# Strassen's algorithm for 14 pairs of the first layer's FFN input, and low parts of its FFN output weights by transfers that add

## The chip, the cores and the metric

The kernel runs on one NeuronCore of a Trainium2 chip. The metric is device microseconds of one execution. Engines are called by their names in the profile: PE (TensorE, matmuls), PEld (its weight loads), DVE (VectorE), ACT (ScalarE), POOL (GpSimd) and SP (SyncE, which issues most transfers). SBUF is the on-chip memory, PSUM the accumulators that PE writes.

## The reference

A trunk of two layers on 512 tokens of width 1024, all in float32. Each layer first mixes tokens (a gated recurrence beside latent attention, about half of the time) and then runs the FFN that this change touches:

```python
mod = (c @ w_ada + b_ada)[:, None, :]
sh_m, sc_m, g_m, sh_f, sc_f, g_f = jnp.split(mod, 6, axis=-1)
...
x = x + g_m * (y @ w_out)
h = rms_norm(x) * (1 + sc_f) + sh_f
gate, up = jnp.split(h @ w_ffn_in, 2, axis=-1)
x = x + g_f * ((jax.nn.silu(gate) * up) @ w_ffn_out)
```

`w_ffn_in` is 1024 x 5632 and `w_ffn_out` 2816 x 1024. The six modulation vectors of a layer come from one conditioning vector `c` and the 1024 x 6144 matrix `w_ada`.

## The kernel before, in words

**Numbers in two parts.** PE multiplies float32 operands at a rounded precision (float32r), so every operand is split in a high part (rounded, by ACT) and a low part (what is left, by DVE), and each product is three matmuls: high by high, high by low, low by high (`mm3`). `split` is the pair of instructions; `w_cols` loads a block of weights, 128 x 1024 floats, from HBM into a `raw` tile and splits it into `whi` and `wlo`. There are three `raw` buffers (`NRAW`) and three pairs of `whi` and `wlo` (`NHL`). In the second layer's FFN output (the argument `dma=last`) `w_cols` already makes the low part in another way: ACT writes minus the high part into `wlo`, and a transfer issued by POOL adds `raw` to it.

**The FFN.** `layer` works on 22 pairs: pair number `fi` is a block of 128 gate columns and the 128 up columns that belong to it. The pairs stand in three blocks (`FCUTS`: pairs 0 to 6, 7 to 13, 14 to 21). Pair 0 (`NAHEAD`) is made ahead, while the norm's statistics are still being computed. The next `NPLAIN[l]` pairs are plain: `gemm_units` makes two units, gate and up, each of 8 x 3 matmuls of 512 columns, and `done_fi` multiplies silu(gate) by up and splits the result into `ah` and `al`. The rest go through `fi_pair`, Strassen's algorithm in Winograd's form: the 2 x 2 blocks are (gate, up) by the two halves of the 1024 inputs on the weight side, and the two halves of the inputs by the two halves of the tokens (`H0`, `H1`, 256 each) on the other. `w_quarters` makes the sums of weights and their splits, `token_halves` the sums of tokens and theirs, once for the whole FFN. A pair is then seven products of 4 x 3 matmuls of 256 columns, between which DVE and ACT read the PSUM accumulators `a`, `b` and `z` and add.

Before the change `NPLAIN` is (21, 5): in the first layer all 21 remaining pairs are plain, and the tokens are prepared by `make_h`; in the second pairs 1 to 5 are plain and 6 to 21 Strassen, and the tokens are prepared by `token_halves`.

The output weights follow by blocks (`fo_block`): while block two's pairs run, the 8 output units of block one (7 x 3 matmuls of 512 columns each) are put between them, while block three's run those of block two, and after the last pair come the 8 units of block three (8 x 3 matmuls each), alone. Each unit ends in an update of the residual `x`.

**Modulation tiles.** A modulation vector is eight tiles: a 512 KB block of `w_ada` is loaded into one of two `graw` buffers, and one DVE instruction multiplies it by `c` and sums. Generators of such tiles stand in the list `background`; each call of `bg()` takes one step. `gemm_units` calls `bg()` after each of its units; `fi_pair` does not. A vector takes nine steps for its eight tiles. In the first layer's FFN the list holds seven vectors (this layer's `G_F`, then the second layer's six), and what is left of it is recorded at once by `drain_bg()` before the last output block. With `BG_GATE` a tile's load waits for the last PE instruction that was recorded before it.

**Order of the work.** The kernel's code only records instructions. `Recorder.order` then simulates them with a table of costs and sets the order of each engine's queue: of the instructions that are ready, the one with the most work still behind it goes first. PE keeps nearly the recorded order. `POOL_DMA` and `POOL_LAT` are this planner's figures for a POOL issue and its landing. Since all instructions are issued at the recorder's end, the profile gives every one the same line, L524; it is read by the names of tiles: `fh`, `fl` (tokens of plain pairs), `xqh`, `xql` (tokens of Strassen pairs), `ws`, `wsh`, `wsl` (sums of weights and their parts), `graw` (modulation tiles).

Of the kernel before, what the change touches and what calls it, by code (L numbers as in the profile page):

```python
# [16 lines left out]
AF = mybir.ActivationFunctionType  # L17
ALU = mybir.AluOpType
# [3 lines left out]
P = 128  # L22
# [3 lines left out]
KD = D // P  # L26
# [6 lines left out]
NF = D_FF // P  # L33
# [33 lines left out]
H0, H1, FULL = slice(0, 256), slice(256, 512), slice(0, 512)  # L67
# [4 lines left out]
NGRAW = 2  # L72
NAHEAD = 1
NLATE = (0, 0)
NPLAIN = (21, 5)
BG_GATE = True
TABLES_AT = 4
SCRIPT = ('x4 x0 d0 d1 x1 m1 x5 x2 n0 n1 g0 g1 x3 b0 r0 p0 b5 g2 e0 m1 m1 g3 q0 g4 s0 e4 b1 q1 a3 t0 g5 a1 p1 q2 w0 v0 a0 y0 m1 s1 m1 s2 x6 m1 e3 x7 w4 e1 b2 t2 g6 m1 q3 a2 m1 e2 s3 r1 b3 v2 m1 g7 p2 m1 q5 e7 w3 t3 q4 w2 m1 v3 e6 w7 b7 m1 s4 a5 w6 y2 a7 a4 m1 p3 e5 q6 a6 t1 w1 s6 s5 m1 b4 v1 y3 t5 m1 t4 q7 t6 v4 s7 b6 v6 m1 t7 y6 v5 w5 v7 y1 y5 y4 y7', 'd0 d1 m1 n0 m1 m1 n1 x1 x0 r0 m1 m1 x2 p0 g0 g1 e0 a0 q1 q0 x3 s1 g2 b0 e2 p1 m1 m1 m1 t1 q2 s0 m1 v1 e1 x4 w0 q3 m1 g3 r1 s2 x5 t0 g4 a1 p3 a2 v0 b6 e4 x7 s3 q6 x6 m1 m1 g5 e5 w2 y0 w4 m1 s6 b1 w1 m1 g6 a4 e6 b2 t3 v3 a6 e3 g7 b3 m1 p2 q7 q5 b7 s7 w3 b5 s5 b4 y1 w6 t6 w5 v6 q4 m1 t5 t2 v2 y6 s4 v5 a3 y2 a5 t4 t7 v4 v7 e7 y3 y5 a7 w7 m1 y4 y7')
# [27 lines left out]
DMA_RUN = 0.6  # L106
DMA_LAT = 2400.0
DMA_ISSUE = 470.0
POOL_DMA = 1200.0
POOL_LAT = 6000.0  # L110
SHORT = 2000.0
TABLE_LOAD = 1300.0
PE_WINDOW = 3413.0
# [424 lines left out]
def trunk(  # L538
# [7 lines left out]
    V, A, T, G, DMA = (  # L546
        rec.engine(e, r)
        for e, r in (("DVE", nc.vector), ("ACT", nc.scalar), ("PE", nc.tensor), ("POOL", nc.gpsimd), ("SP", nc.sync))
    )
# [24 lines left out]
    def f(ap):  # L574
        return ap.bitcast(F32)

    def split(hi, lo, src):
        A.activation(hi, src, AF.Copy)
        V.tensor_tensor(lo, src, f(hi), ALU.subtract)
# [12 lines left out]
    def raw_tile():  # L592
        return rec.tile(wp, [P, 1024], F32, "raw", NRAW, nm("raw"))
# [12 lines left out]
            res.append((hi, lo))  # L606
        return res

    def w_cols(src, nk=KD, raws=None, dma=False):


        raw = raw_tile()
        DMA.dma_start(raw[:, : nk * P], src)
        hi, lo = hl_tiles()
        if dma:
            A.activation(hi[:, : nk * P], raw[:, : nk * P], AF.Copy)
            A.activation(lo[:, : nk * P], f(hi[:, : nk * P]), AF.Copy, scale=-1.0)
            G.dma_start(f(lo[:, : nk * P]), raw[:, : nk * P], accum_op=ALU.add)
        else:
            split(hi[:, : nk * P], lo[:, : nk * P], raw[:, : nk * P])  # L620
        if raws is not None:
            raws.extend(raw[:, k * P : (k + 1) * P] for k in range(nk))
        return [(hi[:, k * P : (k + 1) * P], lo[:, k * P : (k + 1) * P]) for k in range(nk)]
# [61 lines left out]
    for i in range(2):  # L685
        ps, crow, cs = psum("pt"), unit("crow"), slice(i * 512, (i + 1) * 512)
# [189 lines left out]
    def w_quarters(srcs):  # L876

        raws = []
        for src in srcs:
            raw = raw_tile()  # L880
            DMA.dma_start(raw, src)
            raws.append(raw)
        lo_, hi_ = slice(0, 512), slice(512, 1024)
        a11, a12, a21, a22 = raws[0][:, lo_], raws[0][:, hi_], raws[1][:, lo_], raws[1][:, hi_]
        s1, s2, s3, s4 = (unit("ws") for _ in range(4))
        res = {}
        h, l_ = hl_tiles()
        split(h, l_, raws[0])
        res["A11"], res["A12"] = (h[:, lo_], l_[:, lo_]), (h[:, hi_], l_[:, hi_])

        def add(name, s):
            res[name] = unit("wsh", F32R), unit("wsl", F32R)
            split(*res[name], s)

        V.tensor_tensor(s1, a21, a22, ALU.add)
        V.tensor_tensor(s2, s1, a11, ALU.subtract)
        add("S2", s2)
        V.tensor_tensor(s3, a11, a21, ALU.subtract)
        add("S3", s3)
        add("S1", s1)  # L900
        add("A22", a22)
        V.tensor_tensor(s4, a12, s2, ALU.subtract)
        add("S4", s4)
        return res
# [144 lines left out]
    def layer(l, rs, ahead):  # L1049
        last = l == L - 1  # L1050
# [6 lines left out]
        def product(w):  # L1057
            ps = psum("mm")
            for k, (wh, wl) in enumerate(w):
                mm3(ps, wh, wl, hh[k], hl[k], k == 0, k == KD - 1)  # L1060
            return ps
# [9 lines left out]
        if l == 0:  # L1071
            for m in range(3):
                done_down(m, FULL, accs[4 + m])
            ps = accs[NFIRST]
        else:
# [7 lines left out]
            ps = psum("mm")  # L1083
# [30 lines left out]
        xi, v, av, lru_w = {}, {}, {}, {}  # L1114
# [53 lines left out]
        def x_lru(n):  # L1168
            if l == 0 and n < 4:
                ps = unit("xl")  # L1170
                A.activation(ps, accs[n], AF.Copy)
            else:
                ps = product(w_cols(w_in[l, n]))
            convs[n] = conv(n, ps)


# [117 lines left out]
        prs, pts, pos, sas, sbs, yhl = {}, {}, {}, {}, {}, {}  # L1294

        def gate(h, off, res):
            ps = product(w_cols(w_in[l, off + h]))
            res[h] = unit("sg")
            A.activation(res[h], ps, AF.Tanh, scale=0.5)
            if off == OFF_GA:  # L1300
                V.tensor_scalar(res[h], res[h], 1.0, None, ALU.add)
# [19 lines left out]
        yh, yl = [yhl[h][0] for h in range(NH)], [yhl[h][1] for h in range(NH)]  # L1321
# [7 lines left out]
        def done_out(m, cs, ps):  # L1329
# [2 lines left out]
            ahead.add(m, cs)  # L1332

        gemm_units(
            [(m, FULL) for m in range(KD)], yh, yl, lambda m: w_cols(w_out[l, m]), done_out,
        )


# [2 lines left out]
        rs = st.finish(FULL, D, sbuf=True)  # L1341
        na, fast = NAHEAD, NPLAIN[l] + NAHEAD < NF
        pgu, cgu = ahead.units([w_fi[l, c0 + i] for i in range(na) for c0 in (0, NF)])
# [72 lines left out]
            split(ah[fi], al[fi], g)  # L1416

        def w_fi_cols(m):
            return w_cols(w_fi[l, m // 2 + (m % 2) * NF])

        def residual(m, cs, ps):
            V.scalar_tensor_tensor(x[m][:, cs], ps[:, cs], mcol(l, G_F, m), x[m][:, cs], ALU.mult, ALU.add)
# [54 lines left out]
        def fo_block(tiles, ms, done):  # L1477

            k0, nk = tiles[0], len(tiles)
            gemm_units(  # L1480
                ms, [ah[i] for i in tiles], [al[i] for i in tiles],
                lambda m: w_cols(w_fo[l, m, :, k0 * P : (k0 + nk) * P], nk, dma=last), done,
            )


# [75 lines left out]
```

## Time and profile before

| | us |
|---|---|
| median of 3 runs | 1330.85 (1329.75 to 1331.48) |
| the profiled execution | 1330.39 |
| its span, first to last instruction | 1328.6 |
| PE busy | 1309.8 (99%) |
| DVE busy | 945.7 (71%) |
| ACT busy | 676.2 (51%) |
| POOL busy | 235.1 (18%) |
| mean granted TensorE clock | 0.998 |

The first layer's FFN runs from about 328 to 676 us, the second's from about 977 to 1313 us. Matmuls are pipelined: the durations that the profile gives to single ones overlap, so what a group of them takes is read from the length of a stretch and their count, not from their busy times.

### The profile page before, as it was taken

How to read it: one execution, taken by the hardware profiler on the slowest of the kernel's cores; microseconds unless marked ns; L12 is line 12 of the kernel's file. 1: busy time of each engine (PE TensorE's matmuls, PEld its weight loads, DVE VectorE, ACT ScalarE, POOL GpSimd, SP SyncE). 2: the span in 40 equal slices, each digit the busy share in tenths (PEclk: the TensorE clock that was granted, in tenths of full speed). 3: DMA queues.
4: the chain of work that ended last, by engine and by line, in shares of the span. 5: the costliest groups of instructions: out<-in, count | busy, mean ns of one | idle time of the engine just before them, and what ended most of it. 6: DMA issues, size and time to landing. Idle time of an engine off the chain costs nothing.

```text
span 1328.6 us, 18151 instructions
## 1 busy us (share of the span) xinstructions
PE 1309.8 (99%) x6788; PEld 1119.4 (84%) x6788; DVE 945.7 (71%) x1625; ACT 676.2 (51%) x1057; POOL 235.1 (18%) x250
## 2 busy tenths in 40 slices
PE   9999999999999999999999999999999999999997
PEld 7787878888888888888888888888888999899986
DVE  7999887897755555555679886666687766667634
ACT  4597676635322222222356867855474544444532
POOL 0414534314000000000211433312400000000011
PEclk9999999999999999999999999999999999999999
DMA  8744344172655555555414231211333444544473
GB/s 291 237 121 152 117 127 143 64 229 104 220 177 181 172 209 176 183 206 172 147 59 149 94 115 64 96 48 48 106 101 109 133 118 135 155 129 134 126 157 109
DMA packets 56012, 186.44 MB, mean 140 GB/s; under 512 B 7026, under 2 KB 7282, under 8 KB 55924
## 3 DMA queue, kind: packets, MB, share of 16 engines
q1 hardware_dynamic: 52468, 173.75, 39.6%
q0 software_dynamic: 3456, 11.54, 4.7%
q8 instruction: 53, 0.87, 0.3%
q14 instruction: 35, 0.29, 0.1%
HBM read 167.44 MB, written 2.10 MB: 128 GB/s over the span
## 4 chain that ended last, share of the span: by engine, by line
PE 88%; DMA 4%; ACT 3%; DVE 2%; SPq 1%; issue 1%; POOL 0%; DVEq 0%; ACTq 0%
PE mm L524 78%; PE s L524 4%; PE o L524 2%; PE pt L524 2%; DMA raw<-in_w_in_dram 1%; DMA raw<-in_w_ada_dram 1%; SPq L524 1%; DMA graw<-in_w_ada_dram 1%; ACT whi L524 1%; ACT L524 0%; DMA raw<-in_w_ffn_in_dram 0%; DVE raw L524 0%; DMA raw<-in_w_first_dram 0%; DMA crow<-in_c_dram 0%; ACT xc L524 0%
## 5 line engine op out<-in xcount | busy, mean ns | idle before, releaser
L524 ACT ACTIVATE whi<-raw 128x1024 fp32r<-128x1024 f32 (+2 forms) x192 | 199.3, 1038 | 434.6 <-PE mm L524 318.1
L524 DVE TENSOR_TENSOR wlo<-raw,whi 128x1024 fp32r<-128x1024 f32 (+1 forms) x167 | 206.9, 1240 | 103.9 <-ACT whi L524 99.9
L524 PE MATMUL mm<-hl,whi 128*128 128x512 f32 x432 | 168.9, 391 | 0.3 <-DVE hl L524 0.3
L524 PE MATMUL mm<-hh,whi 128*128 128x512 f32 x432 | 166.2, 394 | 1.8 <-ACT ri L524 1.4
L524 PE MATMUL mm<-hh,wlo 128*128 128x512 f32 x416 | 161.8, 390 | 0.0
L524 PE MATMUL mm<-al,whi 128*128 128x512 f32 (+1 forms) x360 | 139.1, 386 | 0.0
L524 PE MATMUL mm<-ah,whi 128*128 128x512 f32 (+1 forms) x360 | 138.9, 386 | 0.0
L524 PE MATMUL mm<-ah,wlo 128*128 128x512 f32 (+1 forms) x360 | 138.5, 385 | 0.0
L524 PE MATMUL mm<-fh,whi 128*128 128x512 f32 x336 | 130.5, 389 | 0.0
L524 PE MATMUL mm<-fh,wlo 128*128 128x512 f32 x336 | 130.5, 389 | 0.0
L524 PE MATMUL mm<-fl,whi 128*128 128x512 f32 x336 | 130.4, 389 | 0.0
L524 PEld LDWEIGHTS mm<-hh,whi 128*128 128x128 f32 x432 | 80.9, 188 | 19.0 <-ACT ri L524 1.5
L524 PEld LDWEIGHTS mm<-hl,whi 128*128 128x128 f32 x432 | 81.2, 188 | 17.4 <-DVE hl L524 1.4
L524 PEld LDWEIGHTS mm<-hh,wlo 128*128 128x128 f32 x416 | 78.1, 188 | 16.0
L524 PE MATMUL mm<-xqh,wsl 128*128 128x256 f32 x320 | 90.4, 283 | 0.0
L524 PE MATMUL mm<-xql,wsh 128*128 128x256 f32 x320 | 90.4, 283 | 0.0
L524 PE MATMUL mm<-xqh,wsh 128*128 128x256 f32 x320 | 90.4, 284 | 0.0
L524 DVE CUSTOM_DVE_ANT_0 graw<-graw,cb,cols 128x1024 f32<-128x1024 f32 x64 | 83.4, 1303 | 6.5 <-DMA graw<-in_w_ada_dram 5.7
L524 POOL TENSOR_SCALAR wsa<-raw,mod 128x128 f32<-128x128 f32 x24 | 17.2, 736 | 388.6 <-PE mm L524 339.4
L524 PEld LDWEIGHTS mm<-ah,whi 128*128 128x128 f32 x360 | 67.7, 188 | 13.2
L524 PEld LDWEIGHTS mm<-ah,wlo 128*128 128x128 f32 x360 | 67.7, 188 | 13.2
L524 PEld LDWEIGHTS mm<-al,whi 128*128 128x128 f32 x360 | 67.7, 188 | 12.6
(257 smaller groups left out, 3055.7 us busy)
## 6 DMA issues: line engine op xcount, KB each, us to landing
graw<-in_w_ada_dram SPq DMA_DIRECT2D x88, 512.0 KB, 4.5
raw<-in_w_ffn_in_dram SPq DMA_DIRECT2D x88, 512.0 KB, 3.4
raw<-in_w_in_dram SPq DMA_DIRECT2D x47, 512.0 KB, 3.4
raw<-in_w_ffn_out_dram SPq DMA_DIRECT2D x32, 448.0 KB, 3.5
raw<-in_w_out_dram SPq DMA_DIRECT2D x16, 512.0 KB, 3.4
raw<-in_w_ffn_out_dram SPq DMA_DIRECT2D x16, 512.0 KB, 3.9
wlo<-raw POOLq DMA_DIRECT2D x16, 448.0 KB, 4.4
raw<-in_w_ada_dram SPq DMA_DIRECT2D x8, 512.0 KB, 4.7
```

What stands on the lines that cost most here:

```text
L524: o.call(*(real(v) for v in o.a), **{k: real(v) for k, v in o.k.items()})
```

## The change

`NPLAIN` goes from (21, 5) to (7, 5): in the first layer pairs 1 to 7 stay plain and pairs 8 to 21 go through `fi_pair`, so the tokens are prepared by `token_halves`. `w_cols` gets a letter for how the low part is made in place of the flag: "v" is `split`, "a" is ACT's negated copy and the transfer that adds. `HOW_FO` is "aa", so the first layer's FFN output now makes its low parts as the second layer's did; all other letters are "v", which is what was there. The branch with `G.tensor_scalar` is used by none. Two figures of the planner change.

```diff
-NPLAIN = (21, 5)
+NPLAIN = (7, 5)
...
-POOL_DMA = 1200.0
-POOL_LAT = 6000.0
+
+HOW_IN = "vv"
+HOW_OUT = "vv"
+HOW_FI = "vv"
+HOW_FO = "aa"
+HOW_A1 = "v"
+POOL_DMA = 900.0
+POOL_LAT = 3700.0
...
-    def w_cols(src, nk=KD, raws=None, dma=False):
+    def split_by(how, hi, lo, src):
+
+
+        if how == "v":
+            split(hi, lo, src)
+            return
+        A.activation(hi, src, AF.Copy)
+        if how == "a":
+            A.activation(lo, f(hi), AF.Copy, scale=-1.0)
+        else:
+            G.tensor_scalar(lo, f(hi), -1.0, 1.0, ALU.mult, ALU.mult)
+        G.dma_start(f(lo), src, accum_op=ALU.add)
+
+    def w_cols(src, nk=KD, raws=None, how="v"):
...
-        if dma:
-            A.activation(hi[:, : nk * P], raw[:, : nk * P], AF.Copy)
-            A.activation(lo[:, : nk * P], f(hi[:, : nk * P]), AF.Copy, scale=-1.0)
-            G.dma_start(f(lo[:, : nk * P]), raw[:, : nk * P], accum_op=ALU.add)
-        else:
-            split(hi[:, : nk * P], lo[:, : nk * P], raw[:, : nk * P])
+        split_by(how, hi[:, : nk * P], lo[:, : nk * P], raw[:, : nk * P])
...
-                lambda m: w_cols(w_fo[l, m, :, k0 * P : (k0 + nk) * P], nk, dma=last), done,
+                lambda m: w_cols(w_fo[l, m, :, k0 * P : (k0 + nk) * P], nk, how=HOW_FO[l]), done,
```

## Rows read from the trace of the kernel before

**Rows 1.** The page: span, busy time by engine, and the copies of high parts.

```profile
span 1328.6 us, 18151 instructions
...
PE 1309.8 (99%) x6788; PEld 1119.4 (84%) x6788; DVE 945.7 (71%) x1625; ACT 676.2 (51%) x1057; POOL 235.1 (18%) x250
...
L524 ACT ACTIVATE whi<-raw 128x1024 fp32r<-128x1024 f32 (+2 forms) x192 | 199.3, 1038 | 434.6 <-PE mm L524 318.1
```

**Rows 2.** Busy time by stretch, the FFN of both layers; PEclk is the granted clock.

```profile
core 0: us, PE busy (x) PEld busy (x) DVE busy (x) ACT busy (x) POOL busy (x), PEclk, DMA share, GB/s
...
327.40:404.20 76.80, 76.80 (x342) 63.48 (x341) 50.63 (x69) 26.69 (x34) 0.00 (x0) 1.00 0.55 186
...
404.20:627.90 223.70, 223.70 (x989) 185.29 (x987) 127.00 (x163) 59.16 (x72) 0.00 (x0) 1.00 0.54 186
...
627.90:676.20 48.30, 48.30 (x215) 40.01 (x214) 33.83 (x40) 19.67 (x27) 15.74 (x22) 1.00 0.42 136
...
964.00:1051.40 87.40, 87.40 (x473) 75.83 (x472) 68.62 (x114) 50.71 (x79) 1.91 (x2) 1.00 0.37 116
1051.40:1160.00 108.60, 107.56 (x744) 100.47 (x743) 75.08 (x126) 53.17 (x86) 6.06 (x7) 1.00 0.48 130
```

**Rows 3.** By stretch: output unit, plain pair; then Strassen pair, output unit.

```profile
404.20:408.96 4.76, 4.76 (x23) 3.94 (x22) 3.72 (x5) 1.60 (x2) 0.00 (x0) 1.00 0.48 170
408.96:419.84 10.88, 10.88 (x50) 9.01 (x49) 4.36 (x5) 2.55 (x4) 0.00 (x0) 1.00 0.47 160
1056.19:1066.26 10.07, 10.07 (x85) 10.05 (x84) 7.26 (x13) 5.05 (x8) 0.85 (x1) 1.00 0.59 178
1066.26:1071.05 4.79, 4.79 (x23) 3.96 (x22) 3.53 (x6) 1.67 (x4) 0.00 (x0) 1.00 0.41 109
```

**Rows 4.** Groups of DVE instructions, 1166.5 to 1265.8 us: busy us, mean ns.

```profile
L524 DVE TENSOR_TENSOR wsl<-ws,wsh 128x512 fp32r<-128x512 f32 x24 | 16.2, 686 | 2.5 <-ACT wsh L524 2.3
L524 DVE TENSOR_TENSOR wlo<-raw,whi 128x1024 fp32r<-128x1024 f32 x6 | 7.3, 1222 | 1.3 <-ACT whi L524 1.0
L524 DVE TENSOR_TENSOR sg<-mm,pq 128x256 f32<-128x256 f32 x13 | 5.5, 424 | 14.0 <-PE mm L524 13.9
L524 DVE SCALAR_TENSOR_TENSOR x<-mm,mod,x 128x512 f32<-128x512 f32 x7 | 5.2, 748 | 2.1 <-PE mm L524 2.1
```

**Rows 5.** Groups of DVE instructions, 404.2 to 513 us: modulation tiles.

```profile
L524 DVE CUSTOM_DVE_ANT_0 graw<-graw,cb,cols 128x1024 f32<-128x1024 f32 x16 | 20.5, 1281 | 1.3 <-DMA graw<-in_w_ada_dram 1.1
```

**Rows 6.** By stretch, columns as in rows 2: output projection, second layer's start, first attention.

```profile
271.80:315.10 43.30, 43.30 (x193) 35.87 (x192) 38.14 (x53) 18.70 (x25) 19.98 (x22) 1.00 0.60 191
...
690.00:750.00 60.00, 59.97 (x290) 49.97 (x289) 56.22 (x102) 42.52 (x69) 9.98 (x8) 1.00 0.41 123
750.00:800.00 50.00, 50.00 (x259) 42.77 (x259) 41.20 (x81) 39.20 (x69) 21.14 (x19) 1.00 0.35 106
...
100.00:225.00 125.00, 118.98 (x580) 98.91 (x580) 108.45 (x208) 87.87 (x149) 56.04 (x46) 1.00 0.42 136
```

**Rows 7.** The chain that ended last, 1140 to 1160 us: start, us, what.

```profile
1145.38 5.77 DMA raw<-in_w_ffn_in_dram
...
1153.87 0.28 ACT pq L524
```

**Rows 8.** Instructions that write `wlo`, 1050 to 1290 us: ns min/median/max; us to landing.

```profile
L524 ACT ACTIVATE wlo<-whi x20: 938/942/1062, 1061.7 to 1288.9; 128x896 fp32r<-128x896 f32 x14, 128x1024 fp32r<-128x1024 f32 x6
L524 POOL DMA_DIRECT2D wlo<-raw x19: 855/862/887, 1063.0 to 1284.5; - x19
...
DMA to landing us min/median/max: 4.2/4.5/7.9
```

**Rows 9.** Loads of modulation tiles, 315 to 650 us: issue ns, first and last start.

```profile
L524 SPq DMA_DIRECT2D graw<-in_w_ada_dram x56: 328/425/437, 317.9 to 636.7; - x56
```

**Rows 10.** The same, 267 to 303 us, beside the first layer's output projection.

```profile
L524 SPq DMA_DIRECT2D graw<-in_w_ada_dram x10: 327/328/426, 267.5 to 294.9; - x10
```

**Rows 11.** The same, 0 to 50 us, the kernel's first products.

```profile
L524 SPq DMA_DIRECT2D graw<-in_w_ada_dram x8: 327/328/430, 6.6 to 39.1; - x8
```

More of the change, by code (lines that the diff above doesn't have):

```diff
@@ L887, in w_quarters @@
         h, l_ = hl_tiles()
-        split(h, l_, raws[0])
+        split_by(HOW_A1, h, l_, raws[0])
         res["A11"], res["A12"] = (h[:, lo_], l_[:, lo_]), (h[:, hi_], l_[:, hi_])
@@ L1172, in x_lru @@
             else:
-                ps = product(w_cols(w_in[l, n]))
+                ps = product(w_cols(w_in[l, n], how=HOW_IN[l]))
             convs[n] = conv(n, ps)
@@ L1296, in gate @@
         def gate(h, off, res):
-            ps = product(w_cols(w_in[l, off + h]))
+            ps = product(w_cols(w_in[l, off + h], how=HOW_IN[l]))
             res[h] = unit("sg")
@@ L1334, in layer @@
         gemm_units(
-            [(m, FULL) for m in range(KD)], yh, yl, lambda m: w_cols(w_out[l, m]), done_out,
+            [(m, FULL) for m in range(KD)], yh, yl, lambda m: w_cols(w_out[l, m], how=HOW_OUT[l]), done_out,
         )
@@ L1418, in w_fi_cols @@
         def w_fi_cols(m):
-            return w_cols(w_fi[l, m // 2 + (m % 2) * NF])
+            return w_cols(w_fi[l, m // 2 + (m % 2) * NF], how=HOW_FI[l])
         def residual(m, cs, ps):
```

## The prediction

> **What bounds the kernel now.** I read the page's first part first: of a span of 1328.6 us TensorE is busy for 1309.8, VectorE 945.7 and ScalarE 676.2 [rows 1]. [...] The second layer's FFN prices what the change adds, since it runs the same functions.
>
> **Step 1, the pairs.** The new setting is 7 plain pairs after the one done ahead, so pairs 8 to 21, 14 of them, go from plain to Strassen. A plain pair is 48 matmuls of 512 columns in 10.88 us (227 ns from start to start); a Strassen pair is 84 of 256 columns in 10.07 us (120 ns) [rows 3]. (The counts in the rows also hold a matmul or two that reach in from either side.) Seven eighths of the columns cost 93% of the time, because each matmul carries some 13 ns beside its columns: from the two rows, 2 x 120 - 227. The gain is 14 x 0.81 = 11.3 us. [...]
>
> **Step 2, the seams.** A block of output units (21 matmuls) takes 4.76 us between plain pairs and 4.79 between Strassen pairs [rows 3]; 16 units between pairs make 16 x 0.03 = +0.5 us.
>
> **Step 3, VectorE in the middle of the FFN.** From the rows a Strassen pair needs on VectorE one split of 1024 (1.22), five splits and four sums of 512 (nine of 0.69), five sums of 256 from PSUM (0.42), and the product and the split of the result (0.69 each): 10.9 us [rows 4]. A plain pair needs two splits of 1024 and two operations of 512: 3.8 us [rows 4]. Each output unit costs one residual update (0.75) [rows 4] and calls one modulation tile of the next layer (1.28) [rows 5]; its split goes away (step 4). A pair and a unit then take 10.9 + 0.75 + 1.28 = 13.0 us of VectorE in 10.07 + 4.79 = 14.9 us of PE: 87%, with 1.9 us to spare. ScalarE stays near half: in the second layer it is at 53.2 of 108.6 us with the same work [rows 2].
>
> How much of that makes PE wait is not shown for this mix, so I bound it. Below: in 690 to 750 us VectorE is 94% busy and PE idle 0.03 us, so 0. Above: in 100 to 225 us VectorE is 87% busy, modulation tiles among its work, and PE idle 6.0 of 125 us, 4.8% [rows 6]; of the 229 us that blocks two and three will take (10.88 + 14 x 10.07 + 16 x 4.79 = 228.4) that is 11.0. The nearest row is the second layer's own Strassen stretch: PE idle 1.0 of 108.6 [rows 2], where the chain runs over a weight tile that took 5.8 us to come and ends at the ScalarE copy that PE wanted, which stood behind that tile's own copies [rows 7]. The added tile can hold a PSUM sum back: between a product and the next into the same accumulator PE has 12 matmuls of cover, 1.44 us, and a sum takes 0.42 plus up to 1.28 of waiting, 1.70. So the 18 tiles called in these blocks cost 0.3 us at most now and then; I take 1.0 for them and 1.0 for the wait that the second layer shows, 2.0 us.
>
> The new preparation of the tokens (8 updates of 0.75, 16 splits, 16 sums of 256: 23.7 us, where 16 updates, 12.0, stood) is hidden: in the second layer PE is busy 87.4 of 87.4 us over it [rows 2], and VectorE in block one, 50.6 of 76.8, takes 12 us more; without that cover it would cost those 12.
>
> **Step 4, low parts by adding transfers.** 24 tiles leave VectorE (24 x some 1.2 us) and take a ScalarE copy of 0.94, a POOL issue of 0.86 and a transfer that lands 4.5 us later, at worst 7.9 [rows 8]. PE sees this only as latency: with the high part's copy (1.04 [rows 1]) the set of buffers is held 7.3 us before PE can use it, plus 5.45 us of use (24 x 227 ns) in the last block. Three sets give 16.35 us; 12.8 fits, and with the worst landing 16.2 still does. Price 0; if the cover went, each of the 24 units would wait by the excess. POOL's issue waits for ScalarE's copy, with the rest of POOL's queue behind it: in blocks two and three that is nothing (POOL is idle there today); in the last block it is the shift sums for the next layer (POOL 15.7 of 48.3 us [rows 2]), which can come later by an issue or two and are read only after the 10.9 us of the units made ahead.
>
> **Step 5, what is late next.** Modulation tiles are called once per GEMM unit, and a Strassen pair makes no such call. 56 tiles belong to this FFN [rows 9]; nine calls bring eight. Today 60 calls come before the last block. After the change there are 2 + 12 + 2 + 16 = 32: three vectors and five tiles, 29, are called there, and the other 27 come in one burst at the last block's start. The burst's pace: 10 issues in 27.4 us, 3.04 us each, beside a fully busy PE [rows 10, 6]. The last block (192 x 0.227 = 43.6 us) and the two units made ahead behind it (10.9) hold 54.5 us, so 18 tiles; their VectorE time, 23 us, fits the 14.5 us idle there today [rows 2] plus the 9.8 of the eight splits that go. SP issues one in some 0.4 us [rows 9], 27 in 11 us, between the weight loads; one that finds its buffer taken holds the loads behind it, which is part of the bound that follows. Nine tiles, 11.5 us, run into the second layer's start, where VectorE has 3.8 us idle to 750 us and 8.8 more to 800 [rows 6]. At best that absorbs all (0); at worst 11.5 - 3.8 = 7.7 us come through. The order ranks a tile by the work that follows it, and these are needed only at the second layer's output projection, so they should fill gaps: nearer 0, I take 2.0.
>
> **Step 6, the planner's figures** for POOL transfers change no operation, only the order, that of the second layer's FFN too: the wait of 1.0 us there may go or another come. -1 to +1, I take 0.
>
> **Sum.** -11.3 + 0.5 + 2.0 + 0 + 2.0 = -6.8 us. The profiled execution took 1330.39 us (span 1328.6 and 1.8 around it), 0.46 under the median of 1330.85. 1330.4 - 6.8 = 1323.6.
>
> **The rivals.**
> A. VectorE becomes the bound in blocks two and three: the idle 1.9 us per pair isn't usable, since it waits on PE in between. For: 87% and 4.8% in the first layer's attention [rows 6]. Against: the same functions at 69% lose 1.0 us in all, and 94% loses nothing elsewhere. Price 11.0 in place of 2.0: 1332.6, no change.
> B. The burst collides with the second layer's start: slower. The mechanism is the tiles' pace. At the kernel's start, with VectorE full, eight issues took 32.5 us, 4.64 each [rows 11]; at that pace 12 tiles fit the 54.5 us and 15 spill, 19.2 us of VectorE, of which 3.8 find room: 15.4 us, so 1330.4 - 11.3 + 0.5 + 2.0 + 15.4 = 1337.0. It decides from 12 spilled tiles on (12 x 1.28 - 3.8 = 11.6, against 8.8 gained before it and 2.7 of margin). For: VectorE is 94% busy from 690 to 750. Against: in the first layer's output projection a burst of ten costs PE nothing, and low-ranked tiles can wait.
> C. Halving the columns costs no more per column: a Strassen pair keeps the full eighth, 10.88 x 7/8 = 9.52 us, the gain is 14 x 1.36 = 19.0, and the time 1330.4 - 19.0 + 4.5 = 1315.9. Against: the second layer's matmuls of a pair start 120 ns apart, not 113, in all of its 16 pairs but at the one wait. 2%. [...]
> D. The pairs don't become Strassen, or buffers keep them apart: the condition in the code is plain, and the second layer's longer stretch fits the same 72 buffers; 1%, 1330.
>
> **How the numbers follow.** Forecast 0.74, range of its own 1318.5 to 1328 (bounds of steps 3, 5 and 6, not all at once); A 0.12, B 0.11, C 0.02, D 0.01. The likeliest time is 1323.5. The range for 8 in 10 takes the forecast's and reaches into A, whose price may be less than its bound: 1318 to 1331. A measurement here tells about 0.2%, 2.7 us, from no change. Faster by more (under 1328.1): the forecast and C, 0.76. Same: D, three quarters of A (0.09) and the mild end of B (0.02), 0.12. Slower: the rest of A (0.03) and of B (0.09), 0.12.
>
> **What would show it.** Right: Strassen pairs of 10.07 us in the first layer from about 415 us on; PE without gaps over 0.5 us there but for one or two; VectorE at 85 to 90% in blocks two and three; 27 modulation tiles after the last output unit between pairs, the last of them between 690 and 750 us; the 24 low parts on the POOL queue landing in 4 to 5 us. Wrong: PE idle over 4 us in blocks two and three with VectorE named (A); PE waits in 680 to 760 us behind VectorE, or raw tiles landing late behind modulation tiles in SP's queue (B); pairs not at 10.07 (C, D).

## The result and the profile after the change

The changed kernel takes 1343.71 us at the median of 6 runs (1340.92 to 1348.2), against 1331.16 before: ratio 1.0092, 95% interval 1.0066 to 1.0119. It is slower by 12.5 us, and 1323.5 was forecast. The profiled execution took 1348.2 us, the longest of the six, so the differences read from it below are at the upper end.

The page of the changed kernel, first lines, as in [rows 1]:

```profile
span 1346.4 us, 19623 instructions
...
PE 1310.3 (97%) x7292; PEld 1139.8 (85%) x7292; DVE 1015.9 (75%) x1807; ACT 739.3 (55%) x1182; POOL 267.8 (20%) x274
```

The span grew by 17.8 us, and PE's share fell from 99 to 97%. To see where, I divided both traces at the first matmul of each kind (tokens of the FFN, the output units behind the last pair, the second layer's own input, its output projection); the lengths are worked out from those starts, to 0.3 us. "Blocks" are the pairs with the output units between them; the "boundary" is the last of those units (4.8 us), the last output block and the units made ahead for the second layer.

| stretch, us | before | after | difference |
|---|---|---|---|
| up to the first FFN (not touched) | 327.8 | 329.9 | +2.1 |
| its blocks one to three | 299.9 | 293.5 | -6.4 |
| boundary: last output block and units made ahead | 61.2 | 76.9 | +15.7 |
| second layer's attention | 231.7 | 237.7 | +6.0 |
| all behind it | 408.0 | 408.5 | +0.5 |

The first line is no effect: in the profiles below whose first stretch has the same instructions and planner figures it lies between 326.6 and 335.5. In this profile 6.8 us of it (11.6 to 18.5) ran at a granted clock of 0.50, in the kernel before none. So the pairs gave 6.4 us, and the boundary and the attention took 21.7.

The same table by stretch as [rows 2, 6], after the change: a Strassen pair of the first layer, then the boundary in two parts, then the second layer's start.

```profile
538.95:549.02 10.07, 10.07 (x86) 10.07 (x85) 7.26 (x12) 5.02 (x8) 0.88 (x1) 1.00 0.51 158
...
623.50:678.00 54.50, 44.90 (x195) 36.24 (x194) 32.37 (x48) 22.72 (x28) 17.51 (x20) 0.93 0.89 256
678.00:700.40 22.40, 20.48 (x87) 16.50 (x85) 18.20 (x31) 8.74 (x14) 7.95 (x9) 0.86 0.77 258
700.40:760.00 59.60, 59.23 (x283) 49.03 (x284) 58.70 (x107) 40.38 (x67) 5.10 (x4) 1.00 0.41 133
760.00:800.00 40.00, 37.21 (x189) 31.96 (x188) 34.16 (x70) 31.20 (x51) 18.58 (x16) 0.96 0.33 104
```

The pair costs what the second layer's cost [rows 3]. In the boundary PE is idle for 9.6 of 54.5 us, the transfers are 89% busy (42% in [rows 2]), and the granted clock, 1.00 before the change, is 0.93 in the first part and 0.86 in the second: it is 0.50 from 670.4 to 680.7 us, from within the long wait to 3.4 us behind it, and once more from 690.9 to 694.3, behind the wait for `sacc`. Who PE waited for, 620 to 800 us (us in total, times, longest):

```profile
PE mm L530 <- DMA wlo<-raw: 9.6, 3, 9.2
PE s L530 <- DVE pl L530: 2.8, 1, 2.8
PE o L530 <- DVE sacc L530: 1.9, 1, 1.9
```

(`sacc` is the sum of squares of the residual, on which the next layer's norm stands; `pl` is the low part of the attention weights.) Nine of these us are one wait, for the low part of the last output unit. POOL's queue shows why it was late (timeline of POOL, 652 to 672 us: start, length, instruction, idle before and releaser):

```profile
653.13 0.89 POOL L530 DMA_DIRECT2D wlo<-raw  x1 [5.09 <-ACT wlo L530]
664.70 2.66 POOL L530 TENSOR_SCALAR wsa<-raw,mod 128x128 f32<-128x128 f32 x4 [10.68 <-DMA raw<-in_w_in_dram]
667.34 2.99 POOL L530 TENSOR_SCALAR wsb<-raw,mod 128x128 f32<-128x128 f32 x3
670.28 0.88 POOL L530 DMA_DIRECT2D wlo<-raw  x1
```

The shift sums for the next layer had been put ahead of the last adding transfer. They waited 10.68 us for their weight tile, behind the modulation tiles' loads, and the transfer, whose copy by ScalarE had ended at 662.4, stood behind them until 670.28, 7.9 us after it was ready. It landed 6.9 us later.

The modulation tiles in 623 to 678 us (issues, then the instruction on VectorE; ns min/median/max), and what VectorE waited for:

```profile
L530 SPq DMA_DIRECT2D graw<-in_w_ada_dram x13: 327/328/1260, 628.7 to 671.5; - x13
L530 DVE CUSTOM_DVE_ANT_0 graw<-graw,cb,bsc x8: 1279/1286/1389, 647.5 to 675.9; 128x1024 f32<-128x1024 f32 x8
L530 DVE CUSTOM_DVE_ANT_0 graw<-graw,cb,cols x5: 1283/1285/1286, 633.1 to 677.4; 128x1024 f32<-128x1024 f32 x5
its engine sat idle before it (us, times) until:
  DMA graw<-in_w_ada_dram: 18.4, 8
...
DMA to landing us min/median/max: 3.6/4.8/8.5
```

Thirteen tiles in 54.5 us, 4.2 us each, where 18 at 3.04 us had been assumed; VectorE stood 18.4 us for loads of tiles that the plan had put at the head of its queue. The boundary as a whole holds 18 tiles (one of them called before it), and the attention ten.

### The profile page after: what moved, and what is told of

Read it like the earlier page. It is cut to its first block, busy times and chain, and to the rows that moved or that the text cites. A ratio compares the mean times of both kernels' runs of the same rounds, so it can differ in the third digit from the quotient of the medians.

```text
span 1346.4 us, 19623 instructions
## 1 busy us (share of the span) xinstructions
PE 1310.3 (97%) x7292; PEld 1139.8 (85%) x7292; DVE 1015.9 (75%) x1807; ACT 739.3 (55%) x1182; POOL 267.8 (20%) x274
## 3 DMA queue, kind: packets, MB, share of 16 engines
q1 hardware_dynamic: 52468, 173.75, 38.0%
q0 software_dynamic: 6912, 23.07, 9.3%
## 4 chain that ended last, share of the span: by engine, by line
PE 69%; DVE 10%; DMA 9%; issue 5%; ACT 4%; POOL 2%; SPq 1%; DVEq 0%; POOLq 0%; ACTq 0%
PE mm L530 61%; PE s L530 4%; DMA raw<-in_w_ffn_in_dram 2%; PE o L530 2%; DMA wlo<-raw 2%; PE pt L530 2%; DVE wlo L530 2%; DMA graw<-in_w_ada_dram 1%; DMA raw<-in_w_in_dram 1%; SPq L530 1%; ACT whi L530 1%; DMA raw<-in_w_first_dram 1%; DVE graw L530 1%; DVE xc L530 1%; DVE ws L530 1%
## 5 line engine op out<-in xcount | busy, mean ns | idle before, releaser
L530 ACT ACTIVATE whi<-raw 128x1024 fp32r<-128x1024 f32 (+3 forms) x178 | 184.2, 1035 | 277.7 <-PE mm L530 182.7
L530 PE MATMUL mm<-xqh,wsh 128*128 128x256 f32 x600 | 170.1, 285 | 2.0 <-DVE pq L530 1.7
L530 PE MATMUL mm<-xql,wsh 128*128 128x256 f32 x600 | 169.5, 283 | 0.0
L530 PE MATMUL mm<-xqh,wsl 128*128 128x256 f32 x600 | 169.4, 283 | 0.0
L530 PE MATMUL mm<-xqh,whi 128*128 128x256 f32 (+1 forms) x432 | 142.7, 331 | 1.1 <-ACT pq L530 1.1
L530 PE MATMUL mm<-xqh,wlo 128*128 128x256 f32 (+1 forms) x432 | 142.3, 330 | 0.0
L530 PE MATMUL mm<-xql,whi 128*128 128x256 f32 (+1 forms) x432 | 142.0, 330 | 0.0
L530 PEld LDWEIGHTS mm<-xqh,wsh 128*128 128x128 f32 x600 | 114.6, 192 | 3.8 <-DVE pq L530 3.3
L530 PEld LDWEIGHTS mm<-xql,wsh 128*128 128x128 f32 x600 | 115.0, 192 | 0.4
L530 PEld LDWEIGHTS mm<-xqh,wsl 128*128 128x128 f32 x600 | 114.9, 192 | 0.0
```

The costliest lines, as they stand in the source:

```text
L530: o.call(*(real(v) for v in o.a), **{k: real(v) for k, v in o.k.items()})
```

## The experiments

Each ran in turn with the kernel before on one chip, and each group (e1 to e4, e5 to e8, e9 to e12, e13 to e18) on another; the median before was 1331.2 to 1332.8 us, so runs are compared by the ratio. Blocks, boundary and attention are the stretches above, from one profiled execution of each run. They can differ by some 3 us with the same work: the attention of e8 and e17 has the same instructions (see e17).

| run | median, us | ratio to before (95%) | blocks | boundary | attention |
|---|---|---|---|---|---|
| before | | | 299.9 | 61.2 | 231.7 |
| changed kernel | 1343.71 | 1.0092 (1.0066 to 1.0119) | 293.5 | 76.9 | 237.7 |
| e1_low_parts_split | 1336.96 | 1.0035 (1.0020 to 1.0050) | 289.4 | 67.3 | 239.4 |
| e2_sums_after_adds | 1350.10 | 1.0139 (1.0114 to 1.0164) | 293.9 | 74.2 | 239.8 |
| e3_no_drain | 1343.08 | 1.0078 (1.0057 to 1.0098) | 292.5 | 68.6 | 239.9 |
| e4_adds_alone | 1334.08 | 1.0018 (1.0001 to 1.0035) | 299.9 | 62.9 | 231.7 |
| e5_burst_alone | 1348.61 | 1.0119 (1.0097 to 1.0142) | 299.9 | 69.9 | 239.3 |
| e6_tiles_back_in_pairs | 1338.86 | 1.0047 (1.0027 to 1.0066) | 305.0 | 61.1 | 232.4 |
| e7_half_the_tiles | 1344.40 | 1.0092 (1.0060 to 1.0124) | 298.6 | 76.8 | 231.9 |
| e8_late_tiles | 1325.97 | 0.9958 (0.9936 to 0.9979) | 289.4 | 60.7 | 238.9 |
| e9_burst_without_loads | 1348.87 | 1.0137 (1.0114 to 1.0159) | 299.9 | 67.5 | 241.9 |
| e10_burst_without_sums | 1333.84 | 1.0011 (0.9994 to 1.0027) | 299.9 | 61.6 | 231.6 |
| e11_plan_slow_loads | 1331.02 | 0.9998 (0.9984 to 1.0012) | 291.5 | 64.7 | 239.7 |
| e12_late_spread | 1331.05 | 0.9996 (0.9979 to 1.0012) | 289.8 | 60.7 | 234.8 |
| e13_burst_planned_long | 1352.09 | 1.0153 (1.0128 to 1.0178) | 301.8 | 64.0 | 236.8 |
| e14_plan_both | 1336.98 | 1.0040 (1.0028 to 1.0053) | 294.5 | 63.6 | 237.6 |
| e15_split_plan_both | 1335.42 | 1.0029 (1.0017 to 1.0042) | 294.3 | 62.0 | 237.3 |
| e16_late_plan_both | 1338.59 | 1.0051 (1.0033 to 1.0069) | 294.9 | 60.7 | 234.8 |
| e17_late_adds | 1333.28 | 0.9998 (0.9980 to 1.0017) | 293.5 | 61.5 | 235.6 |
| e18_late_thin | 1326.54 | 0.9958 (0.9942 to 0.9974) | 289.4 | 60.7 | 234.8 |

**e1_low_parts_split**

```diff
-HOW_FO = "aa"
+HOW_FO = "va"
```

> The changed kernel, but the first layer's output weights get their low parts from VectorE again (HOW_FO "va"); the 14 Strassen pairs and the burst of 27 modulation tiles stay. Theory P (POOL's queue: the last unit's adding transfer stands behind the shift sums, which wait for a late weight tile): with no transfer on POOL the 9.4 us wait in the last block goes, and with it the lower clock behind it; about 1331 to 1334 us, the second layer's attention still 6 us longer than before. Theory B (the burst fills the transfers and VectorE, whoever makes the low parts): the wait only changes its name, to VectorE's low part or to the raw tile; 1340 us or more. Theory V (VectorE is what is short): 24 splits more on VectorE, 95% in blocks two and three, so slower than the changed kernel, 1346 or more.

The long wait goes, and 1336.96 lies between theories P and B, 3 us above P's 1331 to 1334: the boundary is still 6 us too long. What PE waited for, 325 to 1000 us:

```profile
PE s L530 <- DVE pl L530: 4.0, 1, 4.0
PE o L530 <- DVE sacc L530: 3.5, 1, 3.5
```

Theory V falls at once: with VectorE making the low parts of the output units between the pairs too, the blocks gain 10.5 of the 11.3 us, more than with adding transfers.

**e2_sums_after_adds**

```diff
+        last_add[0] = len(rec.ops) - 1
...
+                rec.gate, rec.gate_all = last_add[0], True
                 for k in range(KD):
                     G.tensor_scalar(t, raws[i][k], mcol(self.l, self.ssh, k), 1.0, ALU.mult, ALU.mult)
```

> The changed kernel with one order changed: on POOL the shift sums for the units made ahead are placed after the last adding transfer of the output weights. Burst and adding transfers stay. Theory P: the 9.2 us wait for the low part goes, the last block is back at about 49 us, the time at 1331 to 1335 (the attention's 6 us stay). Theory B: the transfers are 90% busy there all the same, the low part still lands late or the sums do; the last block stays over 55 us, the time over 1339.

Theory P falls. The wait for the low part is 1.6 us, but the boundary still takes 74.2, the run is slower than the changed kernel, and another wait took its place. Who PE waited for, 620 to 710 us:

```profile
PE o L530 <- DVE sacc L530: 5.1, 1, 5.1
PE mm L530 <- DMA wlo<-raw: 1.6, 1, 1.6
```

The 9.2 us wait was the last in a row of late things; without it the boundary is only 2.7 us shorter.

**e3_no_drain**

```diff
             before = list(range(a, b))
-        drain_bg()
+        if last:
+            drain_bg()
```

> The changed kernel without the drain ahead of the first layer's last output block: the 27 modulation tiles left are then called one by one, by the units of the last block and by the second layer's own script. Theory B: last block and boundary go back to about 61 us together, the attention's start loses most of its extra 6 us but takes some tiles instead; 1323 to 1328 us, faster than before the change. Theory P gives the same for the last block (the weight tile is no longer late), so this run tells the burst from Theory V: there the time stays over 1338, because VectorE has the same work.

Not as expected: 1343.08, as Theory V had it, which e1 has refuted. The boundary is back to 68.6 only: eight tiles run in it, one called by each unit of the last block, and PE waits 2.5 us for `sacc` and 1.2 for a low part. Attention takes 239.9: 17 tiles run there, called by the script from its start on, where VectorE was 94% busy [rows 6] and is now 98% (64.8 of 66.2 us). A burst isn't needed; tiles in the wrong place are enough.

**e4_adds_alone**

```diff
-NPLAIN = (7, 5)
+NPLAIN = (21, 5)
```

> No Strassen pairs in the first layer (NPLAIN back to 21), but low parts of its output weights by adding transfers and the new planner figures. 60 calls of modulation tiles come before the last block, so there is no burst. Theory B: nothing waits, 1330 to 1332 us, as before the change. Theory P without the burst as its condition (shift sums stand ahead of the last transfer anyway): the last block waits here too, 1338 us or more.

Attention as before the change, the boundary 1.7 us longer, 0.18% in all. Without left-over tiles nothing breaks, though the shift sums stand ahead of the last adding transfer here too, the transfers are 85% busy in the last block, and VectorE stands 11.6 us for tile loads.

**e5_burst_alone** leaves the pairs plain and the low parts to VectorE (`NPLAIN`, `HOW_FO`), and only keeps the tiles out of the later pairs. The lines that do this:

```diff
-            bg()
+            if not quiet[0]:
+                bg()
...
+                    quiet[0] = l == 0 and fi > 7
```

> No Strassen pairs and no adding transfers in the first layer (NPLAIN 21, HOW_FO "va"), but the units of pairs 8 to 21 call no modulation tile, so that 27 of them are left for the last block and the second layer's start, as in the changed kernel. Theory L (the tiles that are left over cost the time, wherever they come from): the last block and the boundary take 66 to 68 us instead of 61, the second layer's attention 237 to 240 instead of 232; 1341 to 1346 us in all. Theory S (they cost only because Strassen's stretch has left VectorE or the buffers behind): 1330 to 1333, as before the change.

Theory L holds: 16 us slower with not one Strassen pair in the first layer: 8.7 in the boundary, 7.6 in attention. What PE waited for, 620 to 800 us, and VectorE's queue ahead of the first of these waits (timeline):

```profile
PE o L530 <- DVE sacc L530: 3.9, 1, 3.9
PE s L530 <- DVE pl L530: 3.0, 1, 3.0
PE mm L530 <- ACT hh L530: 1.2, 1, 1.2
```

```profile
676.00 1.38 DVE L530 CUSTOM_DVE_ANT_0 graw<-graw,cb,cols 128x1024 f32<-128x1024 f32 x1
677.32 0.08 DVE L530 DVE_READ_ACCUMULATOR2_ANT mod<- 128x1 f32 x1
677.32 0.74 DVE L530 SCALAR_TENSOR_TENSOR x<-mm,mod,x 128x512 f32<-128x512 f32 x1
677.98 1.21 DVE L530 TENSOR_TENSOR wlo<-raw,whi 128x1024 fp32r<-128x1024 f32 x1
679.11 1.77 DVE L530 TENSOR_TENSOR sacc<-sacc,sq 128x512 f32<-128x512 f32 x1
680.81 1.22 DVE L530 SCALAR_TENSOR_TENSOR xw<-x,mod,xh 128x512 fp32r<-128x512 f32 x1
681.95 1.48 DVE L530 CUSTOM_DVE_ANT_0 graw<-graw,cb,cols 128x1024 f32<-128x1024 f32 x1
...
683.37 1.27 DVE L530 CUSTOM_DVE_ANT_0 graw<-graw,cb,cols 128x1024 f32<-128x1024 f32 x1
...
684.57 0.74 DVE L530 SCALAR_TENSOR_TENSOR x<-mm,mod,x 128x512 f32<-128x512 f32 x1
685.24 1.21 DVE L530 TENSOR_TENSOR wlo<-raw,whi 128x1024 fp32r<-128x1024 f32 x1
686.37 0.68 DVE L530 TENSOR_TENSOR sacc<-sacc,sq 128x512 f32<-128x512 f32 x1
```

The queue runs without a gap. Two tiles (681.95 and 683.37) stand between the residual updates `x` at 677.32 and 684.57, and take 2.6 us of the queue; the last `sacc`, for which PE waits, comes behind them. In the same way two tiles at 764.30 and 766.55 us stand ahead of the `pl` that PE waits 3.0 us for. In the last block VectorE has some room left (busy 42.1 of 48.5 us, 630 to 678.5), in the boundary as a whole little: its 59.0 us of work would just fit the 60.9 that the stretch took before, where it had 43.2. What PE loses is more than its wait: the granted clock behind it was 0.84, where the kernel before has 1.00:

```profile
678.50:699.80 21.30, 16.23 (x65) 13.04 (x63) 16.90 (x27) 7.70 (x13) 3.70 (x3) 0.84 0.65 218
```

**e6_tiles_back_in_pairs** and **e7_half_the_tiles** call two tiles, or one, at the end of `fi_pair`.

```diff
             split(ah[fi], al[fi], g)
+            bg(2)
```

> The changed kernel with two calls of modulation tiles after each Strassen pair, so that 60 calls come before the last block again and no burst is left; adding transfers stay. Theory L: attention at 232 us, last block and boundary at 62 to 64; but VectorE needs 10.9 + 0.75 + 3 x 1.28 = 15.5 us in a pair and a unit of 14.9, so blocks one to three take 300 to 304 us; 1333 to 1338 in all. Theory P (adding transfers behind POOL's queue cost the boundary by themselves): last block and boundary stay over 70 us.

> As the run before, but one call after each Strassen pair: some 15 tiles are left over instead of 27, and VectorE needs 14.2 of 14.9 us per pair and unit. Theory L: boundary and attention lose about half of what the changed kernel lost there (16 and 6 us), blocks one to three 294 to 298 us; 1335 to 1340. If a pool of left-over tiles costs only above some number, the boundary is back at 63 and the time near 1330.

e6: boundary and attention are back as expected, adding transfers and all, and now the blocks are 11.5 us longer than the changed kernel's. PE waits there for sums that VectorE (5.5 us) and ScalarE (4.1) read from PSUM, with VectorE busy for 81% of blocks two and three. e7: attention is back, but the boundary isn't halved; the wait of 9.3 us for the last low part is there again. That fits where the tiles run: the attention's ten are gone, but the boundary still holds 16, against 18 in the changed kernel.

**e8_late_tiles** gives VectorE the low parts, takes the tiles out of the last block and puts the second layer's calls (`m1` in its script) into the second half, none among the first 40 steps.

```diff
-HOW_FO = "aa"
+HOW_FO = "va"
...
+        if hold[0]:
+            return
...
-        drain_bg()
+        hold[0] = not last
```

> 14 Strassen pairs, low parts by VectorE, and the 27 left-over tiles held back: none in the last block, none at the second layer's start; they are called one by one in the second half of its attention (800 to 920 us), where VectorE is only some 65% busy, and the last vector in its output projection. Theory L with room on VectorE as the condition: blocks 290 us, last block and boundary 61 to 62, attention 232 to 236; 1321 to 1326, faster than before the change. If tiles cost PE time wherever they stand beside attention (some 0.3 us each), attention takes 240 and the time is 1328 to 1331.

Faster than the kernel before and the changed one: 0.9958. The boundary is 60.7 us; attention still pays 7.2 us in this profile, more than the expected 4, with 19 tiles in it (e17 pays 3.9 for the same).

**e9_burst_without_loads** and **e10_burst_without_sums** split e5's tiles: in e9 VectorE runs its instruction on a tile that is there, with a factor of 0 and no earlier than its load was allowed to start; in e10 the tile is loaded, but only its first 8 columns are summed (0.20 us at the shortest, where 0.1 was expected). Both leave out part of the second layer's modulation.

```diff
+            if rest[0]:
+                rec.gate_all = True
+                V.tensor_tensor_reduce(raw, cb, cb, 0.0, b[:, j : j + 1], ALU.mult, ALU.add, m[:, j : j + 1])
...
+                V.tensor_tensor_reduce(raw[:, :8], raw[:, :8], cb[:, :8], 1.0, b[:, j : j + 1], ALU.mult, ALU.add, m[:, j : j + 1])
```

> The burst alone (no Strassen pairs, no adding transfers), but the 27 left-over tiles are not loaded: VectorE runs the same instruction on a tile that is there, with a factor of 0, so the second layer's last modulation vectors are their biases. Theory Q (in VectorE's in-order queue a tile stands and waits for its late load, and the last updates of the residual behind it): with no load there is nothing to wait for, the last block and the boundary are back at 61 to 63 us; attention keeps most of its 7.6 us more if it is VectorE's work that costs there; 1335 to 1341 in all. Theory W (VectorE's work is what costs, in both places): boundary still 67 or more, 1344 or more.

> The burst alone, but VectorE multiplies and sums only the first 8 of the 1024 columns of each of the 27 tiles (some 0.1 instead of 1.28 us), so the second layer's last modulation vectors leave out the rest. The loads, their buffers and their waits stay. Theory Q: the boundary stays at 65 to 70 us, since the queue waits for loads all the same; attention at 232 to 234; 1338 to 1342. Theory W: both are back, 61 and 232 us, 1331 to 1334.

Theory Q falls twice, and Theory W gives both times. Without loads the boundary is 67.5 and attention 241.9; without the sums 61.6 and 231.6, though VectorE waits longer for loads than in e5 (3.1 us there). In e10, 632 to 700 us:

```profile
DVE graw L530 <- DMA graw<-in_w_ada_dram: 11.2, 11, 2.5
```

Eleven waits, and PE none: in the burst alone it is VectorE's 1.28 us per tile, standing in front of other work, that costs.

**e11_plan_slow_loads**

```diff
-DMA_LAT = 2400.0
+DMA_LAT = 5000.0
```

> The changed kernel with the planner's latency of a load at 5.0 us instead of 2.4, so that it expects the loads as late as the trace shows them (4.7 us at the median and up to 8.5); nothing else. Theory Q: tiles are put later into VectorE's queue, the 21 us that VectorE waits for them shrink by more than half, the last block and the boundary fall from 77 to 62 to 68 us, the time to 1330 to 1338. Theory W: the same work, 1341 or more.

One figure of the planner wins back 12.7 us at the median; in the profiles the boundary falls from 76.9 to 64.7 and attention stays at 239.7. With the figure comes another order: 12 tiles run in the boundary instead of 18, and the shift sums stand behind the last adding transfer. VectorE's waits for tile loads in the boundary fall too, from 21.3 us to 10.0. That they aren't what cost is shown for the burst alone (e9, e10: 3.1 us of them in e5), not for the changed kernel, where adding transfers come on top.

The blocks change as well. Blocks two and three, from the first output unit on, in e17 (adding transfers, the planner's old figure), e11 (adding transfers) and e8 (low parts by VectorE), columns as in [rows 2]:

```profile
403.20:620.50 217.30, 214.30 (x1492) 200.44 (x1491) 160.58 (x272) 104.36 (x167) 14.70 (x17) 1.00 0.59 169
405.90:618.70 212.80, 212.80 (x1493) 200.13 (x1492) 160.54 (x275) 105.75 (x168) 14.69 (x17) 1.00 0.59 172
407.40:620.60 213.20, 213.20 (x1495) 200.48 (x1493) 178.49 (x289) 89.45 (x150) 0.00 (x0) 1.00 0.42 140
```

With e11's order PE has no gap beside the adding transfers; e11 pays 2.5 us in block one instead.

**e12_late_spread** and, last, **e18_late_thin** thin e8's tiles out: vectors that are needed later are called in the output projection and in the second layer's plain pairs.

```diff
-        drain_bg(l)
+        drain_bg(l, SC_F if last else None)
...
+        drain_bg(l, SH_F)
```

> As e8_late_tiles, but only some 10 of the left-over tiles stand in the second half of the second layer's attention, 8 in the output projection behind it and 8 in the plain pairs of its FFN. Theory: with fewer tiles beside attention it loses 2 to 4 us instead of 7; output projection and FFN take theirs without loss; 1321 to 1325. If a tile costs the same wherever it stands, 1325 to 1328 as e8.

> e8 with the held-back tiles placed thinner: never two calls in a row, some 18 in the second half of attention, four and more of the rest in the output projection and the second layer's plain pairs. If tiles cost attention by standing close together (one stop of 4 us at 837 to 844 us in e8): attention 233 to 236, 1322 to 1325. If each costs the same wherever it stands: as e8 or e12, 1325 to 1331.

In e12 attention loses 3.1 us, but the output projection and the FFN's pairs behind it take longer (58.1 and 292.6 us, against 56.8 and 288.7 in e8), and the median is level with before: not as expected. e18, with more tiles in attention but never two in a row, loses 3.1 too and gives back nothing. Its time is e8's, 0.9958, the interval below 1 (0.9942 to 0.9974), so that thinning the tiles out is worth anything isn't shown. In its second half of attention PE has no wait, at 79 and 81% of VectorE (by stretch):

```profile
790.00:850.00 60.00, 60.00 (x292) 50.82 (x291) 47.61 (x85) 49.08 (x74) 26.41 (x21) 1.00 0.39 136
850.00:914.50 64.50, 64.39 (x345) 55.40 (x344) 52.27 (x116) 34.76 (x70) 18.38 (x17) 1.00 0.34 119
```

**e13_burst_planned_long**, **e14_plan_both**, **e15_split_plan_both**, **e16_late_plan_both** change what the planner believes of a tile's length; e14 to e16 have the 5.0 us of e11 too.

```diff
+            if method == "tensor_tensor_reduce" and n == 1024:
+                return 2600.0
```

> The burst alone, as e5, with one figure of the planner changed: it takes a modulation tile's instruction on VectorE for 2.6 us long instead of 1.28. Operations and loads are those of e5. Theory O (the order: the plan puts tiles in front of work that PE waits for, because it thinks that they just fit): with the higher figure fewer stand there, the boundary goes from 70 to 61 to 64 us and attention from 239 to 232 to 236; 1333 to 1339. Theory W in its plain form (there is no room for 27 tiles' work on VectorE in that stretch, in whatever order): boundary and attention together stay 12 us or more over those before the change; 1344 or more.

> The changed kernel with both planner figures: tiles 2.6 us long and loads 5.0 us late. Theory O: blocks one to three stay at 290 to 293 us, boundary 62 to 64, attention 233 to 237; 1322 to 1329, faster than before the change. Theory W: as e11 at best, 1331.

> As e14, with low parts by VectorE ("va") in the first layer's output weights. Theory O: blocks 290 us, boundary 61 to 63, attention 233 to 237, 1321 to 1328. Theory W: as e1, 1336 or more. Against e14 it tells what the adding transfers are worth once the order is right: within 3 us of it if they only move work between engines that both have room.

> As e8 (tiles held back to the second half of attention, low parts by VectorE) with both planner figures. Theory O: attention loses less than the 7 us of e8, 233 to 236, and the time is 1321 to 1325. Theory W: as e8, 1325 to 1328.

Theory O holds by halves. With the same work in all, the burst's boundary falls from 69.9 to 64.0 and its attention from 239.3 to 236.8: two thirds and a third of what the burst costs there is where the plan puts the tiles. In e13 the boundary holds 11 instead of 18, and the attention 17 instead of 10, and yet the attention is shorter: there the place counts, and not the number. But the figure also moves the tiles of the first layer's attention, which in e13 takes 342.6 us up to the FFN instead of 330, and holds up the start of the FFN (a wait of 1.8 us in e13, 2.4 in e14 to e16); all four miss the times of Theory O, and none beats e11 or e8. e14 and e15 differ in the adding transfers alone, by 1.6 us at the median and 0.2 us in the blocks.

**e17_late_adds** is e8 with `HOW_FO = "aa"`.

> e8 with one difference: the low parts of the first layer's output weights come by adding transfers ("aa"), as in the changed kernel. No burst. It prices the adding transfers beside Strassen pairs. If they only take work off VectorE: blocks 289 us as in e8, boundary 61, 1324 to 1327. If they hold weight buffers longer and use the transfer engines twice, as the changed kernel's blocks (293.5 us against 289.4 without) suggest: blocks 292 to 295, boundary 61 to 63, 1329 to 1333.

Blocks 293.5 against 289.4: in this order adding transfers cost 4.1 us beside Strassen pairs, and the time is 0.9998 instead of 0.9958. What PE waited for, 400 to 620 us (e8 has no wait there):

```profile
PE mm L530 <- DVE pq L530: 1.5, 2, 0.9
PE mm L530 <- ACT pq L530: 1.4, 2, 0.8
```

PE waits for sums read from PSUM, not for low parts. How the adding transfers make these late isn't shown; in e11's order they don't.

The attention of e17 has e8's instructions and takes 235.6 instead of 238.9 us. In both PE waits 0.9 and 0.8 us at the same matmuls (838.67 and 840.92 us in e8, 837.85 and 840.10 in e17), but only e8's profile has two stretches of 3.4 us at a granted clock of 0.50; I estimate their cost at half their length, 1.7 us each. Those two in e8, then the whole attention of e17:

```profile
694.30:697.70 3.40, 3.40 (x12) 2.73 (x11) 2.71 (x8) 2.05 (x4) 0.00 (x0) 0.50 0.75 255
841.00:844.40 3.40, 3.40 (x12) 3.21 (x13) 2.24 (x4) 3.06 (x5) 3.07 (x2) 0.50 0.94 337
681.90:917.60 235.70, 233.27 (x1171) 197.11 (x1171) 206.35 (x393) 163.29 (x277) 79.03 (x63) 1.00 0.40 128
```

## Why the prediction was wrong

**Steps 1 and 2 were right.** A Strassen pair takes 10.07 us in the first layer too, and e1's blocks are 10.5 us shorter where 11.3 - 0.5 = 10.8 was worked out. The pair's time from the rows, with an estimated 13 ns per matmul beside its columns, held. PE had no gap in the first layer's FFN before the change [rows 2], and e1 shows that matmul work taken out of it was time.

**Step 3, right in e1, off in the changed kernel.** VectorE beside Strassen pairs was priced at 2.0 us; e1, with even more work on it, loses 0.3 (10.8 - 10.5). The changed kernel loses 4.4 there (10.8 - 6.4), and e17 against e8 puts 4.1 of them down to step 4.

**Step 4 failed: "Price 0".** It reckoned with buffers of split weights and the landing, and there it held: PE's waits in the blocks are for sums from PSUM. e17 against e8 puts the price at 4.1 us in the blocks, with no more than 0.8 in the boundary; the medians differ by 7.3. But it is a price of the plan's order: in e11 blocks two and three lose nothing beside the same transfers. The changed kernel has 9.6 us more in the boundary than e1, where the burst comes together with them. Why the two together cost that isn't settled: e2 takes the long wait away and wins 2.7 of it, and late loads (VectorE stands 21.3 us for tiles, 2.8 in e1) stay a rival that no run here takes away by itself. The step did name POOL's queue, but the wrong way round: it saw shift sums wait for a transfer, and the transfer waited for the shift sums.

**Step 5 failed, and it is what turned the sign.** Its count was right: 27 tiles left over, ten of them in the attention, the last one well inside it, at 826 us. That the boundary holds 18 came out by luck, since it had grown to 76.9 us; the pace was 4.2 us per tile, nearer rival B's 4.64 than the output projection's 3.04 [rows 10, 11]. Above all the price: "they should fill gaps: nearer 0, I take 2.0". e5 measures 16.3 us for this term (8.7 + 7.6). The boundary had no price at all, since VectorE's busy time was seen to fit; the attention costs what the step's own upper bound allowed, 7.7 us (6.0 in the changed kernel, 7.6 in e5), and the step chose the lower end. What it had wrong is that a tile of low rank fills a gap. It is put into any gap that the plan sees, and once it is in VectorE's queue the last residual updates and attention's splits stand behind it (the queue of e5). That the tiles' work on VectorE is the cause is shown by e10, that their place decides by e6, e8 and e13. In the burst alone late loads are not the cause (e9, e10). How much of the rest, a third of the boundary's and two thirds of the attention's, is order that e13's plan didn't mend, and how much is want of room on VectorE, stays open. How far VectorE's longer instructions beside POOL's (below) make a plan wrong that would otherwise hold was not tried.

**Step 6** was right in size: the stretches behind attention differ by 0.5 us.

**The rivals.** B, slower, at 0.11, was the one: burst, pace and sign as it had them, 1337.0 against a median of 1343.7. Its size is in part luck: it put the whole price, 15.4 us, into attention's start, which lost 6.0, and none into the boundary, which lost 15.7. Its pace came near for no good reason: in the stretch that it is read from, 6.6 to 39.1 us, VectorE was busy for 29.1 of 32.5 us and not full, and six more modulation tiles came through `raw` by 45 us, which [rows 11] don't count. A fell: e1 loses 0.3 us in the blocks with more work on VectorE than A had; only the further tiles in e6's and e7's pairs make PE wait there for VectorE's sums by more than 1.5 us (5.5 and 5.2).

## What to carry to other kernels

A call that is tied to a unit of work moves when that unit goes; count where the background work then lands before pricing the unit itself. Spare time of an engine is no room by itself: low-ranked work in an in-order queue delays what comes behind it (by the 2.6 us of two tiles in e5), so price it by the chain that runs there (here the norm's statistics at a layer's end), and put it where no such chain runs. When one queue serves two purposes, ask of each in turn what the other can hold up (here the shift sums held a ready transfer for 7.9 us).

## What the runs showed of the hardware

- In the changed kernel an adding transfer (`q0`) takes the 16 transfer engines about twice as long per byte as what SyncE issues (`q1`), nearly all of it loads. The transfer queues (packets, MB, share of 16 engines over the span):

```profile
q1 hardware_dynamic: 52468, 173.75, 38.0%
q0 software_dynamic: 6912, 23.07, 9.3%
```

  That is 173.75 MB in 512 us of all engines' time (340 MB per ms) against 23.07 MB in 125 us (184).
- In the changed kernel a wait of PE cost more than its length: behind 9.2 us of idle time the granted clock was 0.50 up to 680.7 us, and matmuls of 512 columns started 420 ns apart there (678.25 and 678.67 us) instead of 227. Not every wait did: the same two waits of 0.9 and 0.8 us had 3.4 us at a granted clock of 0.50 behind them in e8's profile and none in e17's, on another chip.
- Some of VectorE's instructions took longer while POOL added two SBUF tiles: the sum of 512 (`sacc`) that takes 0.69 us alone took 1.77 at 679.11 us in e5, and `xw`, the low part of the next layer's input, 1.22 instead of 0.75 at 680.81, both while POOL added the shift sums (678.05 to 682.3 us). The residual update `x`, which reads PSUM, took 0.75 beside such sums too (at 671.37 us in the changed kernel, the sum from 671.77 to 673.03). The change didn't bring this: the kernel before has a `sacc` of 1.77 us too (667.60 us, the sum from 666.69 to 668.83).
